# Moving the scale-and-shift products of the first stage onto the matrix engine, and one gate chunk into another buffer

## The chip, the cores and the metric

The kernel runs on one core of one Trainium2 chip. The metric is the device time of one execution in microseconds (us). The engines of the core work side by side and wait for each other through semaphores: TensorE (PE in the profile; PEld is its weight load), VectorE (DVE), ScalarE (ACT), GpSimd (POOL), and SyncE (SP), which in this kernel only issues transfers (DMAs).

## The reference

One layer of a hybrid backbone: 1024 latent tokens and 128 context tokens, 1024 channels, float32. What matters here is its beginning, and one branch:

```python
mod = silu(cond) @ w_mod + b_mod
shift, scale, gate = split(mod, 3)
h = layernorm(x) * (1 + scale) + shift
proj = h @ w_in                      # q, k, v, z of an attention and a retention branch
...
g = sigmoid(h @ w_gate + b_gate)     # two gates of 1024 channels each
m = ga * oa + gr * orr               # oa, orr: the two branches
out = m @ w_out
y = layernorm(ALPHA * x + gate * out) * ln_g + ln_b
```

`cond` has two rows, one for the latent tokens and one for the context tokens. So scale and shift are two vectors of 1024 each.

## The kernel before, in words

Everything is transposed: the 1152 tokens lie along the free axis, the channels in eight blocks (`KT`) of 128 partitions. `Y` holds h, split into a high and a low part (`Y[:, 0, k]` and `Y[:, 1, k]`), and every matrix multiplication with h or a weight is three float32r products: high by high, low weight by high h, high weight by low h. A weight tile of 128x1024 is split likewise into `whi` (ScalarE, `hi_of`, line 156) and `wlo` (`lo_of`: subtraction on GpSimd, line 185, or on VectorE, line 164). The 1152 tokens are worked in three chunks of 384 columns (`CW`).

Instructions are issued in the order in which the program writes them, on each engine. From `sch.run` on, a planner (`Sched`) chooses the order of several streams from estimated costs (`sch.op`, and `sch.t` for TensorE); the first stage, `phase_h`, is written out by hand. Its order:

1. SyncE's queue loads `cond`, x tile 0, the identity, the bias `bm`, then x tiles 1 to 8 (512 KB each). The tiles use six buffers (`p0x`), two buffers of `pz`, and one weight buffer (`raw`); a later load into a `p0x` buffer waits in the queue until its last reader is done.
2. `stats` (VectorE, with `rstd_of` on GpSimd) and `normalise` (VectorE or ScalarE, the string `by`) per tile. `cond_rows`: TensorE broadcasts silu(cond) over 128 partitions, ScalarE copies it to `scb`.
3. Per tile, eight TensorE transposes into two banks (`tp`), and two ScalarE copies into `xnT`.
4. Scale and shift of a block of 128 channels come in two ways. `by_rows`: VectorE multiplies a 128x1024 weight tile (channels on partitions) by `scb` and sums along the row, for both rows of `cond`; this serves scale blocks 0 and 1 and all eight shift blocks. `scale_k` and `scale_cols`: TensorE multiplies with silu(cond) as a stationary operand of two columns, ScalarE copies the two rows out, TensorE turns them into columns, VectorE adds the bias; this serves scale blocks 2 and 3 (`GS[0]`) and 4 to 7 (`GS[1]`), between or after the other work.
5. The weights of the first two jobs (`first`: q and k of the retention branch's first pair) are split, the low parts on GpSimd.
6. `mod(j)` makes block j of h: ScalarE scales and shifts (`hf`), ScalarE rounds to the high part, GpSimd (block 7: VectorE) subtracts for the low part. `k_part` runs block k's products of both first jobs, all three chunks of both jobs accumulating in six banks.
7. The last two blocks are done per job (`last_parts`). ScalarE copies out the first job's result (`qz`), and the dense stream starts with the next job.

In `phase_a` (retention, and the attention's q, k and v) and `phase_b` (attention, gates, output) the dense stream runs a job per weight tile: each of its three chunks uses one of two banks (`dn`), and its evacuation frees the bank. `g_job` is a gate block: ScalarE applies tanh into a buffer `gt` (two buffers) and the chunk is stored to DRAM. `gate_out` and the rope of `qk_job` use the two buffers `tz`. The first two gate jobs run where `phase_a` ends and `phase_b` begins.

Of the kernel before, what the change touches and what calls it, by code (L numbers as in the profile page):

```python
# [18 lines left out]
P = 128  # L19
# [120 lines left out]
def hybrid_step(ctx: ExitStack, tc: tile.TileContext, I: dict, O: dict):  # L140
# [114 lines left out]
    class Job:  # L255
# [12 lines left out]

        def split(self, eng="p"):
            for i, r in enumerate(self.raw):  # L270
                pool = self.pool2 if i else wp
                h = pool.tile([P, 1024], F32R, tag="whi", name="whi")
                l = pool.tile([P, 1024], F32R, tag="wlo", name="wlo")
                f = hi_of(h, r)
                self.ready = lo_of(eng, l, r, h, f)
                self.hi.append(h)
                self.lo.append(l)
# [81 lines left out]
    def phase_h(first, load_decays):  # L359
# [3 lines left out]
        with es:  # L363
# [21 lines left out]
            def load_wm(kind, j):  # L385
                t = wm[kind, j] = p0x("wm")
                dma(t, I["w_" + kind][j])


            GS = ((2, 4), (4, KT))  # L390

            def load_wk(g, k):

                a, b = GS[g]
                n = 8 // (b - a)
                t = p0x("wk") if (g, k) in ((1, 4), (1, 6)) else p0.tile([P, D], F32, tag="wk", name="wk", bufs=3)
                t = t.rearrange("p (k c) -> p k c", k=n)
                dma(t, I["w_scale_k"][k:k + n, :, (a - 2) * P:(b - 2) * P].rearrange("k p c -> p k c"))
# [38 lines left out]
            def by_rows(kind, j):  # L437

                d = m1 if kind == "scale" else sh
                for r in range(2):  # L440
                    v_stt(junk, wm[kind, j], 1.0, scb[r], ALU.mult, ALU.mult, accum_out=d[:, j, r:r + 1])
                if kind == "scale":
                    v_ts(d[:, j, :], d[:, j, :], bm[:, 8 + j:9 + j], 1.0, ALU.add, ALU.add)
                else:
                    v_ts(d[:, j, :], d[:, j, :], bm[:, j:j + 1], None, ALU.add)
# [3 lines left out]
            def scale_k(g, k):  # L449

                n = (GS[g][1] - GS[g][0]) * P
                if k == 0:
                    scale_ps[g] = psum_now("tp")
                mm(scale_ps[g][0:2, :n], sc[:, k, :], wm[g, k], k == 0, k == KT - 1)

            def scale_cols(g):
                a, b = GS[g]
                rows = p0.tile([2, 512], F32, tag="rows", name="rows")
                act(rows[:, :(b - a) * P], scale_ps[g][0:2, :(b - a) * P])
                tp = psum_now("tp")  # L460
                for j in range(b - a):
                    nc.tensor.transpose(tp[:, 2 * j:2 * j + 2], rows[:, j * P:(j + 1) * P], ident[0:2, 0:2])
                    sch.t += 0.107
                v_stt(m1[:, a:b, :], tp[:, 0:2 * (b - a)].rearrange("p (j r) -> p j r", r=2), 1.0,
                      bm[:, 8 + a:8 + b].rearrange("p (j o) -> p j o", o=1).to_broadcast([P, b - a, 2]),
                      ALU.add, ALU.add)
# [66 lines left out]
            def k_part(n, k, part):  # L533
                hi, lo = vw[n]
                for c in range(NC):
                    ps, cs = acc[n][c][:, :CW], slice(c * CW, (c + 1) * CW)
                    if part == 0:
                        mm(ps, hi[0][:, k, :], Y[:, 0, k, cs], k == 0, False)
                        mm(ps, lo[0][:, k, :], Y[:, 0, k, cs], False, False)
                    else:  # L540
                        mm(ps, hi[0][:, k, :], Y[:, 1, k, cs], False, k == KT - 1)

            for k in range(KT - 2):
                mod(k + 1)
                for part in range(2):
                    for n in range(2):
                        k_part(n, k, part)
                if k < 3:
                    for q in range(3 * k, min(3 * k + 3, KT)):
                        scale_k(1, q)  # L550
                if k == 2:
                    scale_cols(1)
# [4 lines left out]
        def last_parts(n):  # L557
            for k in (KT - 2, KT - 1):
                for part in range(2):
                    k_part(n, k, part)  # L560
# [412 lines left out]
    def phase_b():  # L973
# [584 lines left out]
def _layout(a):  # L1558
# [13 lines left out]
    out["w_scale"] = wm[:, D:D + 2 * P].T.reshape(2, P, D)  # L1572
# [55 lines left out]
```

## Time and profile before

| | |
|---|---|
| median of 3 runs | 1702.33 us (1699.15 to 1705.84) |
| profiled execution | 1701.82 us, of which the span is 1700.0 us |
| TensorE busy | 1654.5 us (97%) |
| VectorE, ScalarE, GpSimd busy | 856.3, 609.6, 813.1 us |
| chain that ended last | PE 80%, DVE 6%, DMA 5%, POOL 3%, ACT 2% of the span |

The span is the time from the first to the last recorded instruction; the time of the execution also has what lies around it. "Busy" counts an engine's instructions, "idle before" is the engine's idle time ahead of an instruction and what ended it. The chain is found by going back from the last instruction, at each step to what released it. The stretches view gives, for each stretch, its length, then the busy time (and number of instructions) of PE, PEld, DVE, ACT and POOL, the clock granted to TensorE as a share of full speed, the busy share of the transfer engines and GB/s.

### The profile page before, as it was taken

What the parts mean: (1) busy time and instruction counts of PE and PEld (TensorE: products, weight loads), DVE (VectorE), ACT (ScalarE), POOL (GpSimd) and SP (SyncE); (2) the same over time, 40 slices, a digit from 0 to 9 for tenths busy, and PEclk for the clock granted to TensorE, in tenths of its full rate; (3) what the DMA queues carried; (4) which work ended last, traced back from release to release, by engine and by line L of the source; (5) the groups of instructions that cost most, each with busy time, mean ns of one, the idle gap of its engine ahead of it and who ended that gap; (6) DMA issues with size and microseconds to landing.
All of it is one profiled execution on the core that took longest, in us unless ns stands there. A gap on an engine that the chain in (4) does not pass through costs nothing.

```text
span 1700.0 us, 27027 instructions
## 1 busy us (share of the span) xinstructions
PE 1654.5 (97%) x10495; PEld 1609.5 (95%) x10495; DVE 856.3 (50%) x1681; ACT 609.6 (36%) x1138; POOL 813.1 (48%) x555
## 2 busy tenths in 40 slices
PE   6899999999999999999999999999999999999998
PEld 5699999999999999999999999999999999999886
DVE  8545506413714626665555665666565124134676
ACT  5632222121221235555555555555545220012200
POOL 4547417444634637664847475656656322112200
PEclk8999999999999999999999999999999999999999
DMA  7435412430341365443535353525242578854432
GB/s 274 149 100 147 131 46 86 132 116 23 100 127 44 112 204 161 152 144 113 169 97 172 92 167 93 170 95 165 75 158 73 202 273 282 260 174 137 160 125 87
DMA packets 135185, 237.36 MB, mean 140 GB/s; under 512 B 15801, under 2 KB 103313, under 8 KB 134033
## 3 DMA queue, kind: packets, MB, share of 16 engines
q1 hardware_dynamic: 135056, 235.63, 43.4%
q8 instruction: 83, 1.36, 0.3%
q14 instruction: 46, 0.37, 0.1%
HBM read 161.08 MB, written 74.49 MB: 139 GB/s over the span
## 4 chain that ended last, share of the span: by engine, by line
PE 80%; DVE 6%; DMA 5%; issue 3%; POOL 3%; ACT 2%; SPq 1%; DVEq 0%; POOLq 0%; ACTq 0%
PE dn L149 53%; PE S L149 8%; PE o L149 6%; PE e L149 6%; PE tp L153 4%; PE a L149 4%; DMA gt<-Gd 2%; DVE junk L173 1%; SPq L203 1%; DMA wm<-in_w_shift 1%; ACT E L156 1%; PE tp L149 1%; DVE st L181 1%; DVE eps L173 1%; POOL wlo L185 1%
## 5 line engine op out<-in xcount | busy, mean ns | idle before, releaser
L149 PE MATMUL dn<-Y,whi 128*128 128x384 f32 x3200 | 834.3, 341 | 8.7 <-ACT Y L156 2.8
L149 PEld LDWEIGHTS dn<-Y,whi 128*128 128x128 f32 x3200 | 568.1, 189 | 14.7 <-ACT Y L156 4.0
L149 PE MATMUL dn<-Y,wlo 128*128 128x384 f32 x1600 | 537.5, 336 | 0.7 <-DVE wlo L164 0.7
L185 POOL TENSOR_TENSOR wlo<-raw,whi 128x1024 fp32r<-128x1024 f32 x87 | 210.9, 2428 | 444.8 <-ACT whi L156 444.5
L149 PEld LDWEIGHTS dn<-Y,wlo 128*128 128x128 f32 x1600 | 301.5, 188 | 1.0 <-DVE wlo L164 1.0
L1067 DVE TENSOR_REDUCE nm<-S 128x1 f32<-128x1152 f32 x144 | 178.1, 1237 | 180.4 <-PE S L149 180.0
L189 POOL TENSOR_SCALAR E<-E,r 128x640 f32<-128x640 f32 x64 | 142.8, 2231 | 126.8 <-DVE r L173 86.2
L156 ACT ACTIVATE E<-S,nm 128x1152 f32<-128x1152 f32 x144 | 162.4, 1128 | 79.4 <-DVE nm L1067 73.5
L149 PE MATMUL dn<-whi,Y 128*128 128x256 f32 x864 | 157.4, 283 | 2.4 <-ACT rt L156 1.0
L149 PEld LDWEIGHTS dn<-whi,Y 128*128 128x128 f32 x864 | 134.1, 189 | 3.3 <-ACT rt L156 1.4
L149 PE MATMUL o<-wTh,V 128*128 128x256 f32 x576 | 133.6, 290 | 0.1
L156 ACT ACTIVATE wTh<-tp 128x512 fp32r<-128x512 f32 (+1 forms) x168 | 88.7, 544 | 111.4 <-PE tp L153 107.7
L156 ACT ACTIVATE whi<-raw 128x1024 fp32r<-128x1024 f32 x88 | 92.1, 1055 | 85.0 <-PE dn L149 84.8
L149 PE MATMUL dn<-wlo,Y 128*128 128x256 f32 x432 | 121.3, 281 | 0.0
L164 DVE TENSOR_TENSOR wTl<-tp,wTh 128x512 fp32r<-128x512 f32 (+1 forms) x168 | 99.7, 613 | 24.9 <-ACT wTh L156 24.9
L185 POOL TENSOR_TENSOR E<-E 128x640 f32<-128x640 f32 x64 | 100.9, 1576 | 5.3
L149 PE MATMUL S<-K,QH 128*128 128x384 f32 (+1 forms) x400 | 94.6, 340 | 5.8 <-ACT E L156 5.8
L149 PEld LDWEIGHTS o<-wTh,V 128*128 128x128 f32 x576 | 99.3, 188 | 0.5 <-ACT wTh L156 0.4
L149 PE MATMUL S<-K,QL 128*128 128x384 f32 (+1 forms) x400 | 92.5, 334 | 0.0
L153 PE MATMUL tp<-ident,E 128*128 128x128 f32 x584 | 86.8, 272 | 0.0
L173 DVE SCALAR_TENSOR_TENSOR gt<-gt,dn 128x384 f32<-128x384 f32 x48 | 26.6, 554 | 117.9 <-DMA gt<-Gd 64.7
L169 DVE TENSOR_SCALAR KD<-tp,kdec 128x256 f32<-128x256 f32 (+1 forms) x48 | 16.0, 408 | 138.5 <-PE tp L153 138.5
(197 smaller groups left out, 2504.4 us busy)
## 6 DMA issues: line engine op xcount, KB each, us to landing
K<-Kd SPq DMA_DIRECT2D x8, 1280.0 KB, 7.9
Gd<-gt SPq DMA_DIRECT2D x48, 192.0 KB, 2.3
V<-Vd SPq DMA_DIRECT2D x24, 384.0 KB, 3.6
gt<-Gd SPq DMA_DIRECT2D x48, 192.0 KB, 2.5
Y<-OAd SPq DMA_DIRECT2D x16, 576.0 KB, 4.2
raw<-in_w_gate SPq DMA_DIRECT2D x16, 512.0 KB, 4.0
QH<-Qh SPq DMA_DIRECT2D x64, 128.0 KB, 3.1
QL<-Ql SPq DMA_DIRECT2D x64, 128.0 KB, 2.9
```

Of the source, the lines that this page charges most:

```text
L149: nc.tensor.matmul(out, lhsT=lhsT, rhs=rhs, start=start, stop=stop)
L153: nc.tensor.transpose(out, in_, ident)
L156: nc.scalar.activation(out, in_, func, **kw)
L164: nc.vector.tensor_tensor(out, a, b, op=op)
L169: nc.vector.tensor_scalar(out, a, s1, s2, op0=op0, **kw)
L173: nc.vector.scalar_tensor_tensor(out, a, s, b, op0=op0, op1=op1, **kw)
L181: nc.vector.bn_stats(out, a)
L185: nc.gpsimd.tensor_tensor(out, a, b, op=op)
L189: nc.gpsimd.tensor_scalar(out, a, s1, None, op0=op0)
L203: nc.sync.dma_start(out=out, in_=in_)
L1067: nc.vector.tensor_reduce(nm[:, m:m + 1], ps[:, :nb, :kw], axis=AX.XY, op=ALU.max, negate=True)
```

## The change

The order of the first loads, the place where the first blocks' scale and shift are computed, who splits and subtracts, and one buffer:

- `w_mod01` is a new layout of the input: scale and shift of blocks 0 and 1 side by side, 512 columns, with the contraction index on partitions. Its four tiles are loaded between the x tiles. `cond` is loaded behind x0, the identity and the bias behind x1.
- `GS` now has three groups: the 512 columns of `w_mod01`; scale 2 and 3; scale 4 to 7. Group 0's `scale_k` products stand between the transposes of tiles 1 to 6, its `scale_cols` behind tile 6. Groups 1 and 2 stand behind the first part of blocks 0 and 1.
- `by_rows` is left for the shifts of blocks 2 to 7.
- `split` is divided into `split_hi` and `split_lo`. The first jobs' low parts, and all low parts of h, are computed by VectorE.
- Block 0's scaling is done on VectorE, in four pieces; its high part in three.
- `k_part` has three parts instead of two (the low weight's products are now a part of their own).
- The decay parameters are loaded at block 2.
- In `g_job`, the middle chunk of the first two gate jobs uses a `tz` buffer.

```diff
+        def split_hi(self, i=0):
+            self.hi.append((self.pool2 if i else wp).tile([P, 1024], F32R, tag="whi", name="whi"))
+            self.ready = hi_of(self.hi[i], self.raw[i])
+
+        def split_lo(self, eng="p", i=0):
+            self.lo.append((self.pool2 if i else wp).tile([P, 1024], F32R, tag="wlo", name="wlo"))
+            self.ready = lo_of(eng, self.lo[i], self.raw[i], self.hi[i], self.ready)
...
-            GS = ((2, 4), (4, KT))
+            GS = ((0, 4), (0, 2), (2, 6))
...
-                t = p0x("wk") if (g, k) in ((1, 4), (1, 6)) else p0.tile([P, D], F32, tag="wk", name="wk", bufs=3)
+                t = p0x("wk") if k == 6 or g == 1 else p0.tile([P, D], F32, tag="wk", name="wk", bufs=3)
...
+            load_x(0)
             dma(cond, I["cond"])
-            load_x(0)
+            load_x(1)
             dma(ident, I["ident"])
             dma(bm, I["b_mod"])
-            for i in range(1, NTILE):
+            load_wk(0, 0)
+            for i in range(2, NTILE):
                 load_x(i)
+                if i in (2, 4, 6):
+                    load_wk(0, i)
...
+                for k in ((), (0, 1), (2,), (3,), (4,), (5,), (6, 7), (), ())[i]:
+                    scale_k(0, k)
+                if i == 6:
+                    scale_cols(0)
+                if i == 7:
+                    first[0].split_hi()
                 if i == 2:
-                    load_wm("scale", 0)
-                    load_wm("shift", 0)
                     first[0].load()
                     first[1].load()
-                    for k in range(0, KT, 4):
-                        load_wk(0, k)
-                    load_wm("scale", 1)
-                    load_wm("shift", 1)
-            first[0].split()
-            first[1].split()
-            for k in range(KT):
-                scale_k(0, k)
-            load_wm("shift", 2)
-            for k in range(0, KT, 2):
-                load_wk(1, k)
-            load_decays()
-            by_rows("scale", 0)
-            by_rows("shift", 0)
-            later_loads = [("shift", j) for j in range(3, KT)]
+                    load_shift(2)
+                    load_wk(1, 0)
+                    load_wk(1, 4)
+                    load_shift(3)
+                    for k in range(0, KT, 2):
+                        load_wk(2, k)
 
             def mod(j):
                 hf = pz.tile([P, NT], F32, tag="o_sb", name="hf", bufs=2)
-                for r, (a, b) in enumerate(((0, NL), (NL, NT))):
-                    act(hf[:, a:b], xnT[:, j, a:b], AF.Identity, scale=m1[:, j, r:r + 1], bias=sh[:, j, r:r + 1])
-                hi_of(Y[:, 0, j, :], hf)
-                lo_of("p" if j < KT - 1 else "v", Y[:, 1, j, :], hf, Y[:, 0, j, :])
-                if j + 2 < KT:
-                    by_rows("shift", j + 2)
-                    if later_loads:
-                        load_wm(*later_loads.pop(0))
-
-            by_rows("scale", 1)
-            by_rows("shift", 1)
+
+                def affine(c0, c1, r):
+                    x, m, b = xnT[:, j, c0:c1], m1[:, j, r:r + 1], sh[:, j, r:r + 1]
+                    if j:
+                        act(hf[:, c0:c1], x, AF.Identity, scale=m, bias=b)
+                    else:
+                        v_ts(hf[:, c0:c1], x, m, b, ALU.mult, ALU.add, fast=True)
+
+                if j:
+                    affine(0, NL, 0)
+                    affine(NL, NT, 1)
+                    hi_of(Y[:, 0, j, :], hf)
+                else:
+                    affine(0, CW, 0)
+                    affine(CW, 2 * CW, 0)
+                    first[0].split_lo("v")
+                    affine(2 * CW, NL, 0)
+                    affine(NL, NT, 1)
+                    for c in range(NC):
+                        hi_of(Y[:, 0, j, c * CW:(c + 1) * CW], hf[:, c * CW:(c + 1) * CW])
+                    first[1].split_hi()
+                    first[1].split_lo("v")
+                if 2 <= j < KT - 2:
+                    by_rows(j + 2)
+                lo_of("v", Y[:, 1, j, :], hf, Y[:, 0, j, :])
+                if j < 2:
+                    by_rows(j + 2)
+                if j in (0, 2):
+                    load_shift(2 * j + 4 - j)
+                    load_shift(2 * j + 5 - j)
+                if j == 2:
+                    load_decays()
+
             mod(0)
-            scale_cols(0)
...
             for k in range(KT - 2):
                 mod(k + 1)
-                for part in range(2):
+                for part in range(3):
                     for n in range(2):
                         k_part(n, k, part)
-                if k < 3:
-                    for q in range(3 * k, min(3 * k + 3, KT)):
-                        scale_k(1, q)
-                if k == 2:
-                    scale_cols(1)
+                    if part == 0 and k < 2:
+                        for q in range(KT):
+                            scale_k(k + 1, q)
+                        scale_cols(k + 1)
...
         def g_job(j):
             def evac(c, ps):
-                t = pz.tile([P, CW], F32, tag="gt", name="gt", bufs=2)
+                if j < 2 and c == 1:
+                    t = pz.tile([P, CW], F32, tag="tz", name="gt", bufs=2)
+                else:
+                    t = pz.tile([P, CW], F32, tag="gt", name="gt", bufs=2)
...
-    out["w_scale"] = wm[:, D:D + 2 * P].T.reshape(2, P, D)
+    out["w_mod01"] = np.concatenate([wm[:, D:D + 2 * P], wm[:, :2 * P]], axis=1).reshape(8, P, 4 * P)
```

More of the change, by code (lines that the diff above doesn't have):

```diff
@@ L267, in load @@
                 self.raw.append(r)
-        def split(self, eng="p"):
[L270 to L277, printed above, removed]
+        def split_hi(self, i=0):
[4 more added lines that the diff above has]
+            self.ready = lo_of(eng, self.lo[i], self.raw[i], self.hi[i], self.ready)
+        def split(self, eng="p"):
+            for i in range(len(self.raw)):
+                self.split_hi(i)
+                self.split_lo(eng, i)
         def views(self):
@@ L383, in load_x, with load_shift @@
                 xt.append(t)
-            def load_wm(kind, j):
-                t = wm[kind, j] = p0x("wm")
-                dma(t, I["w_" + kind][j])
-            GS = ((2, 4), (4, KT))
+            def load_shift(j):
+                t = wm["shift", j] = p0x("wm")
+                dma(t, I["w_shift"][j])
+            GS = ((0, 4), (0, 2), (2, 6))
             def load_wk(g, k):
@@ L395, in load_wk @@
                 n = 8 // (b - a)
-                t = p0x("wk") if (g, k) in ((1, 4), (1, 6)) else p0.tile([P, D], F32, tag="wk", name="wk", bufs=3)
+                t = p0x("wk") if k == 6 or g == 1 else p0.tile([P, D], F32, tag="wk", name="wk", bufs=3)
                 t = t.rearrange("p (k c) -> p k c", k=n)
-                dma(t, I["w_scale_k"][k:k + n, :, (a - 2) * P:(b - 2) * P].rearrange("k p c -> p k c"))
+                dma(t, I["w_scale_k" if g else "w_mod01"][k:k + n, :, a * P:b * P].rearrange("k p c -> p k c"))
                 for i in range(n):
                     wm[g, k + i] = t[:, i, :]
+            load_x(0)
             dma(cond, I["cond"])
-            load_x(0)
+            load_x(1)
             dma(ident, I["ident"])
             dma(bm, I["b_mod"])
-            for i in range(1, NTILE):
+            load_wk(0, 0)
+            for i in range(2, NTILE):
                 load_x(i)
+                if i in (2, 4, 6):
+                    load_wk(0, i)
             junk = p0.tile([P, D], mybir.dt.bfloat16, name="junk")
@@ L435, in cond_rows, with by_rows @@
                     act(scb[r][:, g * 512:(g + 1) * 512], ps)
-            def by_rows(kind, j):
-                d = m1 if kind == "scale" else sh
+            def by_rows(j):
                 for r in range(2):
[L441 to L445, printed above, removed]
+                    v_stt(junk, wm["shift", j], 1.0, scb[r], ALU.mult, ALU.mult, accum_out=sh[:, j, r:r + 1])
+                v_ts(sh[:, j, :], sh[:, j, :], bm[:, j:j + 1], None, ALU.add)
             scale_ps = {}
@@ L452, in scale_k @@
                 if k == 0:
-                    scale_ps[g] = psum_now("tp")
+                    scale_ps[g] = psum_now("tp" if g else "dn")
                 mm(scale_ps[g][0:2, :n], sc[:, k, :], wm[g, k], k == 0, k == KT - 1)
             def scale_cols(g):
-                a, b = GS[g]
+                n = GS[g][1] - GS[g][0]
                 rows = p0.tile([2, 512], F32, tag="rows", name="rows")
-                act(rows[:, :(b - a) * P], scale_ps[g][0:2, :(b - a) * P])
+                act(rows[:, :n * P], scale_ps[g][0:2, :n * P])
                 tp = psum_now("tp")
-                for j in range(b - a):
+                for j in range(n):
                     nc.tensor.transpose(tp[:, 2 * j:2 * j + 2], rows[:, j * P:(j + 1) * P], ident[0:2, 0:2])
                     sch.t += 0.107
-                v_stt(m1[:, a:b, :], tp[:, 0:2 * (b - a)].rearrange("p (j r) -> p j r", r=2), 1.0,
-                      bm[:, 8 + a:8 + b].rearrange("p (j o) -> p j o", o=1).to_broadcast([P, b - a, 2]),
-                      ALU.add, ALU.add)
+                for j0, dst, a, m, one in (((0, m1, 0, 2, 1.0), (2, sh, 0, 2, 0.0)), ((0, m1, 2, 2, 1.0),),
+                                           ((0, m1, 4, 4, 1.0),))[g]:
+                    c0 = 8 + a if one else a
+                    v_stt(dst[:, a:a + m, :], tp[:, 2 * j0:2 * (j0 + m)].rearrange("p (j r) -> p j r", r=2), one,
+                          bm[:, c0:c0 + m].rearrange("p (j o) -> p j o", o=1).to_broadcast([P, m, 2]),
+                          ALU.add, ALU.add)
             def normalise(i):
@@ L538, in k_part @@
                         mm(ps, hi[0][:, k, :], Y[:, 0, k, cs], k == 0, False)
+                    elif part == 1:
                         mm(ps, lo[0][:, k, :], Y[:, 0, k, cs], False, False)
@@ L558, in last_parts @@
             for k in (KT - 2, KT - 1):
-                for part in range(2):
+                for part in range(3):
                     k_part(n, k, part)
```

## The prediction

> **What bounds the kernel now.** I read the page's first part, then the busy time by stretches, the chain of work that ended last, and each engine's timeline of the first stage. The page first, then stretches (PE busy first; granted clock, DMA share and GB/s last):
>
> ```profile
> span 1700.0 us, 27027 instructions
> PE 1654.5 (97%) x10495; PEld 1609.5 (95%) x10495; DVE 856.3 (50%) x1681; ACT 609.6 (36%) x1138; POOL 813.1 (48%) x555
> ...
> 0.00:75.10 75.10, 55.96 (x268) 41.67 (x269) 58.49 (x91) 41.88 (x56) 39.81 (x35) 0.93 0.57 208
> 200.00:400.00 200.00, 199.22 (x1404) 198.43 (x1403) 58.66 (x162) 47.58 (x94) 78.93 (x56) 1.00 0.30 93
> ```
>
> TensorE is the bound: between 200 and 400 us it is busy 199.22 of 200. In the first 75.10 us it is busy only 55.96, so some 19 us of waiting stand there. Only removed TensorE waiting, or slow TensorE time, can shorten the kernel. Two places hold it. The chain (start, us, what):
>
> ```profile
> 35.75 13.42 DMA wm<-in_w_shift
> ...
> 603.60 7.32 DMA Gd<-gt
> ```
>
> The first stage is led by VectorE's row products (`junk`) and by late loads of their weights; at 603.60 the first gate chunk's store holds its buffer. The timelines (start, duration; in brackets the idle time before and what ended it):
>
> ```profile
> 5.30 6.15 PE L149 MATMUL a<-ident,sc 128*128 128x128 f32 x32 [5.30 <-DMA ident<-in_ident]
> 18.95 3.14 PE L153 MATMUL tp<-ident,xt 128*128 128x128 f32 x16 [0.52 <-ACT xnT L156]
> 25.74 1.14 PE L153 MATMUL tp<-ident,raw 128*128 128x128 f32 x8 [0.20 <-ACT xnT L156]
> 27.08 3.62 PE L149 MATMUL tp<-wk,sc 128*2 128x256 f32 x16 [0.20 <-ACT xnT L156]
> 35.23 0.69 PE L149 MATMUL dn<-Y,whi 128*128 128x384 f32 x1
> 41.15 2.74 PE L149 MATMUL tp<-wk,sc 128*2 128x512 f32 x6
> 67.69 0.33 PE L149 MATMUL dn<-Y,wlo 128*128 128x384 f32 x1
> 67.86 0.33 PE L149 MATMUL dn<-Y,whi 128*128 128x384 f32 x1
> 80.51 0.44 PE L149 MATMUL dn<-Y,wlo 128*128 128x384 f32 x1 [0.69 <-DVE wlo L164]
> ...
> 7.78 1.29 DVE L181 BATCH_NORM_STATS2 st<-xt 128x6 f32<-128x512 f32 x2 [1.27 <-DMA xt<-in_x]
> 9.23 0.76 DVE L169 TENSOR_SCALAR xt<-xt,mv,rs 128x1024 f32<-128x1024 f32 x1
> 29.52 2.18 DVE L169 TENSOR_SCALAR sh<-sh,bm 128x2 f32<-128x2 f32 x1
> 31.62 1.21 DVE L173 SCALAR_TENSOR_TENSOR junk<-wm,scb 128x1024 bf16<-128x1024 f32 x1
> 32.88 3.25 DVE L173 SCALAR_TENSOR_TENSOR junk<-wm,scb 128x1024 bf16<-128x1024 f32 x1
> 73.19 1.36 DVE L164 TENSOR_TENSOR Y<-hf,Y 128x1152 fp32r<-128x1152 f32 x1 [3.25 <-ACT Y L156]
> 79.23 1.22 DVE L164 TENSOR_TENSOR wlo<-raw,whi 128x1024 fp32r<-128x1024 f32 x1 [4.69 <-ACT whi L156]
> ...
> 21.28 1.23 ACT L156 ACTIVATE xt<-xt,rs 128x1024 f32<-128x1024 f32 x1
> 26.43 1.09 ACT L156 ACTIVATE xnT<-tp 128x512 f32<-128x512 f32 x2 [0.26 <-PE tp L153]
> 27.41 1.99 ACT L156 ACTIVATE whi<-raw 128x1024 fp32r<-128x1024 f32 x2
> 31.80 1.62 ACT L156 ACTIVATE hf<-xnT,sh,m 128x1024 f32<-128x1024 f32 x2 [2.40 <-DVE sh L169]
> 33.46 1.16 ACT L156 ACTIVATE Y<-hf 128x1152 fp32r<-128x1152 f32 x1
> 56.16 0.59 ACT L156 ACTIVATE rows<-tp 2x512 f32<-2x512 f32 x1 [0.95 <-PE tp L149]
> 75.09 1.98 ACT L156 ACTIVATE qz<-dn 64x384 f32<-64x384 f32 x4 [1.93 <-PE dn L149]
> ...
> 28.54 6.50 POOL L185 TENSOR_TENSOR wlo<-raw,whi 128x1024 fp32r<-128x1024 f32 x2 [4.98 <-ACT whi L156]
> ```
>
> Read in order: the transposes end at 26.9 (25.74 + 1.14), but the first projection starts only at 35.23. Between lie the row products for block 0's scale and shift, the shift's bias add (2.18 us beside GpSimd's split, where another product takes 1.21 alone and 3.25 beside one), 1.62 of scaling, 1.16 of high part. Projections are spaced 67.86 - 67.69 = 0.17 us. The stage's end is q's first evacuation at 75.09; the next job's weights then follow on ScalarE and VectorE (1.22 at 79.23), and the stream starts at 80.51.
>
> **The change, part by part.** *Loads.* The same 27 tiles of 512 KB, in another order: the four tiles of scale and shift 0 and 1 stand among the x tiles. Clock and transfer rows:
>
> ```profile
> 17.00:19.00 2.00, 1.48 (x9) 1.05 (x7) 1.97 (x6) 1.98 (x4) 1.04 (x3) 0.51 1.03 410
> 21.00:23.00 2.00, 1.07 (x8) 0.60 (x6) 1.81 (x4) 2.00 (x4) 1.16 (x3) 1.00 1.08 353
> 35.00:37.00 2.00, 2.00 (x7) 1.98 (x8) 1.96 (x3) 0.00 (x0) 2.00 (x2) 0.50 0.05 2
> 60.00:63.00 3.00, 0.57 (x5) 0.25 (x3) 2.93 (x6) 2.87 (x4) 0.01 (x1) 1.00 0.00 0
> ...
> 609.00:611.60 2.60, 0.00 (x1) 0.00 (x0) 0.00 (x0) 0.58 (x2) 0.00 (x0) 0.87 1.03 381
> 611.60:613.00 1.40, 1.35 (x4) 1.35 (x5) 0.00 (x0) 1.40 (x2) 0.38 (x1) 0.50 0.50 179
> 617.00:618.00 1.00, 1.00 (x5) 1.00 (x4) 0.00 (x0) 0.00 (x0) 0.00 (x0) 0.61 1.15 312
> ```
>
> At 410 GB/s a tile takes 1.28 us. x1 lands at 7.78 (the DMA wait ends there); the last x tile is now the 13th, so 7.78 + 11 x 1.28 = 21.9. Its statistics (1.29 and the aggregation) end at 23.4, which hides in what follows. SP's queue now stops at the fourth of these tiles until x0 is transposed (about 15), with x7, x8 and both first weights behind it; what is queued ahead (seven x and three weight tiles) keeps the transfers busy to about 17, and x7 joins the queue before it runs dry: nil to 0.5 us, my estimate. `ident` moves behind x1, from 5.30 to about 7.7 (x1's landing, which no longer waits for `ident`'s 64 KB); that delays the conditioning broadcasts, 6.15 us ending at 11.45 now, to 13.85. It costs 2.4 us of TensorE time before transpose 0, and I count all of it. `cond` moves behind x0; `sc` is still ready before `ident`. `load_decays` and shifts 4 to 7 go later on SP, needed first after the stage.
>
> *Scale and shift 0, 1 on TensorE.* Six products at 41.15 took 2.74 and belong to three k: spaced 0.43, so 0.87 per k of 512 columns. Eight k add 6.9 us between the transposes. Removed: eight 256-wide k (3.62 at 27.08) and eight 1.21 us row products, with their reads and bias adds about 10.2 us of VectorE. TensorE chain: transposes 1.05 a tile; 13.85 + seven tiles 7.4 + 6.9 + waits for evacuations 0.2 ends at 28.3. Then `scale_cols`: copy 0.59, four small transposes 0.4, two tiny VectorE adds, with hand-offs to 29.8; its accumulator lies in a bank of `dn` that nothing wants yet. Behind these adds on VectorE stands tile 8's normalisation (0.76 to 30.55), behind the column transposes those of tile 7. Tile 7's and 8's transposes end 31.65; ScalarE's whi split (half of 1.99, now ahead of tile 8's evacuation) and 1.09 evacuation end 33.2. Covered by this: the ScalarE normalisations (1.23).
>
> *Block 0 in pieces.* VectorE scales the first 768 columns, and splits q's weights, while ScalarE evacuates. A 1024 piece takes 0.76, so 384 about 0.35. After 33.2 only one 384-wide high part remains, 0.5 (a third of 1.16 and overhead): first projection at 33.75, against 35.23, with 2.1 us idle before it. Later pieces and k's weight split keep the second half until 35.75.
>
> *From there TensorE leads.* 144 projections in the stage, 18 of them after its critical point: 126 x 0.1735 = 21.9 us. Second scale group 3.5, third 7.0, each with a copy and column transposes and hand-offs (0.75 and 1.1), 1.2 us of waits in block 0: 35.4 in all, end 33.75 + 35.4 = 69.2. VectorE is next: it gets eight low parts of 1.36 and two of 1.22 from GpSimd, and has six shifts' products (about 2.5 each) left, now alone on its memory (the 3.25 shrinks to 1.21). The third group's columns come at 33.75 + 24 projections 4.2 + 10.5 + hand-offs and waits 3.1 = 51.6; from 52, three shifts 7.5 and five low parts 6.8 make 66.3, and the last low part, which waits for ScalarE's high part, ends near 68; it is needed at 69.0. The second group's scales stand on VectorE behind the row products of shifts 2 and 3, so block 2 starts on ScalarE only at 45; the third group's 7.0 us on TensorE, to 51, cover that. So what VectorE takes over from GpSimd costs nothing as long as this 1 us holds; without it, 1 to 2 us. Loads of shift 5 wait for row product 2 (41) and land by 45, needed 52. ScalarE has 2.8 per block against 3.1 of projections.
>
> q's evacuation then starts at 69.3 instead of 75.09: gain 5.8. What follows keeps its length (80.51 - 75.09 = 5.42). Bounds: 1.5 if the stage keeps its length from the first projection on (33.75 against 35.23); with `ident` arriving as before, 8.2.
>
> *Gate chunk in z's buffer.* ScalarE and TensorE there:
>
> ```profile
> 600.72 0.58 ACT L156 ACTIVATE gt<-dn,bg 128x384 f32<-128x384 f32 x1 [1.87 <-PE dn L149]
> 611.02 0.58 ACT L156 ACTIVATE gt<-dn,bg 128x384 f32<-128x384 f32 x1 [9.72 <-DMA Gd<-gt]
> ...
> 611.65 1.01 PE L149 MATMUL dn<-Y,whi 128*128 128x384 f32 x2 [2.65 <-ACT gt L156]
> ```
>
> Chunk 2 needs chunk 0's buffer, whose store lands at 610.9 (603.60 + 7.32). TensorE idles 2.65, and its clock then stands at 0.50 to past 617: some 5.8 us at half rate, 2.9 lost. With chunk 1 in `tz` (rope, its last reader, comes ahead of the gate chunks), chunk 2 takes the second `gt` as soon as it is computed, 24 projections after chunk 1: 600.7 + 4.2 = 604.9. The next job's first chunk still waits until 611 for chunk 0's store, but TensorE has the other bank to fill to 613. Gain 2.65 + 2.9 = 5.5. Bounds: 0, if another store is then the late one, to 5.5.
>
> Sum against the profiled execution's 1701.82 us (1700.0 span and 1.82 around it; 0.5 under the median 1702.33): -5.8 - 5.5 = 1690.5. The order of later work can shift, since it is planned from costs that change here; where, as between 200 and 400, almost nothing idles, it has little to win or lose, and I allow 2 us either way.
>
> [...] From 18.95 to 22.1 only transposes ran, and the clock went from 0.51 to 1.00. [...]
>
> **Rivals.** *1. A cold start of the projections.* No TensorE work from 30.7 (27.08 + 3.62) to about 35 left the clock at 0.50 at 35.00:37.00, 2.65 us did so at 609, while 60.00:63.00 (0.57 busy of 3.0) kept 1.00. My gap is 2.1 us. If it drops, about 6 us run at half rate: 3 lost, 1693.5. [...]
>
> *2. The gate wait stays*, for another late store: transfers are near saturation there (1.03). Then -5.8 alone: 1696.0. For it: 7.32 us for one store. Against: chunk 2's buffer is untouched until then.
>
> *3. Slower: the clock stays at half from the transposes to block 1.* Place: TensorE's chain, 13.85 to 54. At half rate the 2-column products cost 17.4 more, 72 transposes 4.0 (3.14/16 = 0.196 at 18.95 against 1.14/8 = 0.14), 36 projections 5.3: +27, so 1701.8 + 27 - 11 = 1718. It decides once the extra passes 11 us, that is when the third scale group is cold as well. Against: the products at 27.08, right behind transposes, took 3.62/16 = 0.226, the same per column as those at 41.15; at half the clock it would be 0.45.
>
> *4. The stage gains nothing*, because hand-offs between VectorE, ScalarE and TensorE that I set too short, or loads, make up the 5.8: 1696.3.
>
> **How the numbers follow.** Forecast 0.50 (1688 to 1693.5); rival 1 0.20; rival 2 0.15; rival 4 0.10; rival 3 0.05. 0.5% is 8.5 us, the least that a measurement of this kernel can tell from no change: the line is 1693.8. Faster: 0.50 and half of rival 1, 0.60; slower: 0.05; same 0.35. Range: 1686 (`ident` as early as now and the later order 2 us better: 1690.5 - 2.4 - 2) to 1698 (rival 2 or 4 with the order 2 us worse).
>
> **What would show it.** First projection near 33.8, no GpSimd split before 70, first q evacuation near 69.3, stream start near 74.7; clock 1.00 from 21 us on; no idle TensorE behind the first gate job's `gt`, and clock 1.00 after it. The forecast is wrong if `scale_cols` holds VectorE's queue (tile 8) much past 30, if the projections of blocks 0 and 1 are spaced 0.32, or if VectorE's last low part ends past 69.

## The result, and the profile after

| | before | after |
|---|---|---|
| median, side by side | 1700.9 us (1698.74 to 1705.84, 6 runs) | 1692.26 us (1690.51 to 1694.42, 6 runs) |
| profiled execution | 1701.82 us, span 1700.0 | 1694.42 us, span 1692.6 |

The ratio is 0.9947, 95% interval 0.9931 to 0.9962: faster by 0.53%, 8.6 us, at the edge of the half per cent that the prediction took as its line. The forecast was 1690.5 us, in 1686 to 1698. The profiled execution is the slowest of the six after; what that hides comes below. Of the kernels further down, one run of the gate edit alone (e3) took 2715.07 us at a mean granted clock of 0.556 and is in no ratio. The page of after and its stretches, as shown of before (PE busy first; granted clock, DMA share and GB/s last):

```profile
span 1692.6 us, 27051 instructions
PE 1654.4 (98%) x10515; PEld 1605.9 (95%) x10515; DVE 845.0 (50%) x1676; ACT 608.2 (36%) x1139; POOL 784.5 (46%) x546
...
0.00:70.00 70.00, 58.28 (x288) 39.43 (x289) 47.80 (x86) 40.45 (x57) 11.60 (x26) 0.98 0.64 227
13.00:33.00 20.00, 17.11 (x89) 8.35 (x87) 13.67 (x32) 15.13 (x27) 5.89 (x12) 1.00 1.04 393
33.00:35.00 2.00, 1.34 (x4) 0.83 (x5) 0.61 (x1) 2.00 (x3) 0.00 (x0) 0.81 1.02 389
35.00:37.00 2.00, 2.00 (x7) 0.67 (x6) 2.00 (x3) 1.97 (x3) 0.00 (x0) 0.50 0.14 54
37.00:39.00 2.00, 2.00 (x9) 0.67 (x8) 1.97 (x3) 0.07 (x1) 0.00 (x0) 0.83 0.00 0
609.00:611.60 2.60, 2.60 (x17) 2.60 (x16) 1.30 (x1) 1.85 (x3) 1.35 (x1) 1.00 1.00 356
720.00:725.00 5.00, 2.43 (x13) 2.11 (x12) 0.56 (x1) 2.67 (x5) 3.44 (x3) 0.87 0.60 208
725.00:730.00 5.00, 5.00 (x26) 4.91 (x26) 2.55 (x4) 2.30 (x5) 0.50 (x1) 0.78 0.00 0
```

TensorE's busy time is what it was (1654.4 against 1654.5), so on balance the 7.4 us of span are waiting that went. The first stage is 58.28 busy in 70. From 13 to 33 us the clock is 1.00, with nothing but transposes and two-column products until the first projection at 32.45; between 33 and 39 it falls to 0.50; at 609 TensorE no longer waits; at 720 to 730 there is a new loss. The timelines of the first stage (start, duration; idle time and its end in brackets):

```profile
7.03 5.39 PE L149 MATMUL a<-ident,sc 128*128 128x128 f32 x32 [7.03 <-DMA ident<-in_ident]
14.68 1.88 PE L149 MATMUL dn<-wk,sc 128*2 128x512 f32 x4
29.64 1.14 PE L153 MATMUL tp<-ident,raw 128*128 128x128 f32 x8 [0.23 <-ACT xnT L156]
32.45 0.86 PE L149 MATMUL dn<-Y,whi 128*128 128x384 f32 x2 [1.67 <-ACT Y L156]
35.67 4.58 PE L149 MATMUL tp<-wk,sc 128*2 128x256 f32 x16
75.33 0.44 PE L149 MATMUL dn<-Y,wlo 128*128 128x384 f32 x1 [0.64 <-DVE wlo L164]
...
28.55 0.80 DVE L169 TENSOR_SCALAR raw<-raw,mv,rs 128x1024 f32<-128x1024 f32 x1
67.28 1.36 DVE L164 TENSOR_TENSOR Y<-hf,Y 128x1152 fp32r<-128x1152 f32 x1 [1.63 <-ACT Y L156]
...
69.96 1.98 ACT L156 ACTIVATE qz<-dn 64x384 f32<-64x384 f32 x4 [2.71 <-PE dn L149]
...
76.38 4.77 POOL L185 TENSOR_TENSOR wlo<-raw,whi 128x1024 fp32r<-128x1024 f32 x2 [8.05 <-ACT whi L156]
```

The transposes end at 30.78, the first projection starts at 32.45 (35.23 before), the stream at 75.33 (80.51 before): a lead of 5.18. At 14.68 stand two k of the scale products, between transposes; no GpSimd split comes before 76.38. The first gate job, after, on ScalarE:

```profile
593.47 0.56 ACT L156 ACTIVATE gt<-dn,bg 128x384 f32<-128x384 f32 x1
600.10 0.58 ACT L156 ACTIVATE gt<-dn,bg 128x384 f32<-128x384 f32 x1 [3.58 <-PE dn L149]
```

Chunk 2 follows at 600.10, where before it waited for the store until 611.02. Matching the same instruction in both traces gives the lead along the kernel (ScalarE's gate chunk and softmax rows):

| instruction | before, us | after, us | lead |
|---|---|---|---|
| stream start | 80.51 | 75.33 | 5.18 |
| first gate chunk | 598.28 | 593.47 | 4.81 |
| first softmax | 620.85 | 610.33 | 10.52 |
| softmax rows at about 696 and 734 us of after | | | 10.73, then 7.75 |
| end of the span | 1700.0 | 1692.6 | 7.4 |

So 10.7 us were won by 700 us, close to the 11.3 of the sum, and 3.0 were lost at one place, 722 us. Behind it smaller steps nearly cancel: 1.3 more went at 990 us, and 1.0 came back between 1440 and 1500. The chain of waits, SyncE, ScalarE and TensorE there:

```profile
713.96 8.26 DMA ORd<-goh
...
713.27 0.59 SPq L203 DMA_DIRECT2D K<-Kd  x1
...
722.24 0.49 ACT L156 ACTIVATE goh<-dn 128x384 f32<-128x384 f32 x1 [2.68 <-DMA ORd<-goh]
723.98 1.33 PE L149 MATMUL S<-K,QH 128*128 128x384 f32 x3 [2.57 <-ACT E L156]
```

A chunk of the retention branch's gated output (`gate_out`; "the reset gate" in the expectations below) is stored from a `goh` buffer; there are two. The store was issued 0.7 us behind the 1280 KB load of the third head's K, and landed after 8.26 us. ScalarE's copy into that buffer waited 2.68, the softmax behind it on ScalarE's queue was late, TensorE idled 2.57 us, and its clock went to 0.87 and 0.78 in the two rows above. Before has the same order and the same wait, smaller:

```profile
724.66 6.74 DMA ORd<-goh
...
730.00:735.00 5.00, 3.95 (x26) 3.60 (x25) 1.45 (x3) 2.94 (x6) 4.13 (x4) 1.00 0.71 239
```

There the store took 6.74, TensorE lost about 1.05 of the 5 us at 730 to 735, and the clock stayed at 1.00. So about half of the 3.0 us is the longer wait (2.57 - 1.05 = 1.5), and the rest is the slow clock behind it.

### The profile page after: what moved, and what is told of

Same layout as the page of the kernel before. It is cut to its first block, busy times and chain, and to the rows that moved or that the text cites. A ratio compares the mean times of both kernels' runs of the same rounds, so it can differ in the third digit from the quotient of the medians.

```text
span 1692.6 us, 27051 instructions
## 1 busy us (share of the span) xinstructions
PE 1654.4 (98%) x10515; PEld 1605.9 (95%) x10515; DVE 845.0 (50%) x1676; ACT 608.2 (36%) x1139; POOL 784.5 (46%) x546
## 4 chain that ended last, share of the span: by engine, by line
PE 86%; issue 3%; DVE 3%; DMA 3%; POOL 3%; ACT 2%; SPq 0%; DVEq 0%; POOLq 0%; ACTq 0%
PE dn L149 56%; PE S L149 8%; PE o L149 6%; PE e L149 6%; PE a L149 5%; PE tp L153 5%; PE tp L149 1%; DMA gt<-Gd 1%; ACT E L156 1%; DMA Vd<-vh 1%; POOL wlo L185 1%; DMA ORd<-goh 0%; SPq L203 0%; DVE eps L173 0%; DMA RSd<-rst 0%
## 5 line engine op out<-in xcount | busy, mean ns | idle before, releaser
L185 POOL TENSOR_TENSOR wlo<-raw,whi 128x1024 fp32r<-128x1024 f32 x85 | 204.5, 2409 | 434.5 <-ACT whi L156 432.3
```

What stands on the lines that cost most here:

```text
L185: nc.gpsimd.tensor_tensor(out, a, b, op=op)
```

## The experiments

Each kernel is compared with runs of the kernel before on the same chip. These gave medians of 1699.43 us (e1 to e4), 1700.58 (e5 to e8) and 1702.32 (e9 to e12, on another chip), so kernels of different groups are compared by their ratios and not by their times. Theory: two gains, 5 to 6 us in the first stage and 5 to 6 at the gate, which add up, less what a transfer takes back at 722 us. Rival: one of them is the whole gain, or the first stage's lead is lost on the way.

**The changed kernel again, and each half alone.**

> The changed kernel once more, as it is. Theory: 1692 us, ratio 0.993 to 0.996. In its first profile the lead over the kernel before was 10.5 us at the first softmax (610 us) and 7.4 us at the end; 3 us went at 722 us (a store of the gated output took 8.3 us, TensorE idled 2.6 us and its clock fell) and at 990 us. The order of the instructions there is that of the kernel before. Theory A: such a loss belongs to one execution; the second profile has another pattern and a lead nearer 9 to 11 at the end. Rival B: it comes from the shifted transfers and is there again, 2.6 us of TensorE waiting for E near 722.

1692.21 us, ratio 0.9957 [0.9945, 0.9969]. The profiled execution has the loss at 722 us once more (store 8.48 us, TensorE idle 2.79), as rival B said.

```diff
 # e2: this edit, in the changed kernel; e3: the kernel before, with the lines marked - in place of the one marked +
-                if j < 2 and c == 1:
-                    t = pz.tile([P, CW], F32, tag="tz", name="gt", bufs=2)
-                else:
-                    t = pz.tile([P, CW], F32, tag="gt", name="gt", bufs=2)
+                t = pz.tile([P, CW], F32, tag="gt", name="gt", bufs=2)
```

> The changed kernel with both gate jobs' middle chunks back in gt: the first stage's part alone. Theory (two gains that add): stage lead 5.2 at the stream's start (75.3 us), TensorE again idle 2 to 3 us at the third gate chunk and at half clock behind it; 5.5 us slower than the changed kernel, 1697.5 us, ratio 0.997. Rival: the wait at the gate came from the old timing of the first stage and does not return: 1692, ratio 0.995.

> The kernel before with the gate edit alone. Theory: the wait of 2.65 us and the half clock behind it go, nothing else: 5.5 us faster than before, 1695.5 us, ratio 0.9968. Rival (another store is the next late one): 0 to 2.7 us faster.

The first stage alone: 1700.89 us, ratio 1.0001 [0.999, 1.0012], nothing, where 0.997 was expected. The gate edit alone: 1696.48 us, 0.9978 [0.9969, 0.9988], some 3.7 us, where 0.9968 was expected, just outside this interval. In e3's trace the lead goes from -0.7 at the first gate chunk to +5.0 at the first softmax: 5.7 us, the predicted 5.5. In e2's, the stage's lead is there at the gate (593.78, 4.5 ahead), and goes in two steps:

```profile
608.36 1.01 PE L149 MATMUL dn<-Y,whi 128*128 128x384 f32 x2 [3.82 <-ACT gt L156]
...
721.16 8.73 DMA ORd<-goh
...
731.66 1.33 PE L149 MATMUL S<-K,QH 128*128 128x384 f32 x3 [3.05 <-ACT E L156]
```

The wait for the gate chunk's buffer is 3.82 instead of 2.65, which leaves 3.3 of the lead; and at 722 to 732 the store takes 8.73, TensorE idles 3.05 and its clock falls: the lead goes from 3.5 to -1.1. The two halves don't add in the medians: 0 and 3 us alone, 7 to 9 together.

**The identity early.** The prediction counted 2.4 us for the later identity.

```diff
-            load_x(0)
             dma(cond, I["cond"])
-            load_x(1)
+            load_x(0)
             dma(ident, I["ident"])
+            load_x(1)
```

> The changed kernel with the identity loaded behind x0 again, and cond first, x1 and the bias behind them. Theory (TensorE's chain leads the transposes, and the identity starts it): identity at 5.3 instead of 7.0, first projection 1 to 1.7 us earlier (near 31), the kernel 1 to 2 us faster than the changed one, ratio 0.994. Rival (the x tiles' landing leads, as VectorE's waits of 0.2 to 0.7 us for them say): first projection as now at 32.4, 1692 us.

1691.91 us, ratio 0.995 [0.9938, 0.9962]. The identity is there at 5.17 (7.03), yet the first projection comes at 31.99, only 0.46 earlier, closer to the rival: VectorE now waits 1.40 us for x tile 2 (0.68 in after), so the tiles' arrival, more than the identity, sets the pace. The stream starts at 74.75. The lead is 10.9 at the first softmax and stays at 11.1 past 722 us:

```profile
713.52 6.83 DMA ORd<-goh
...
722.11 0.79 PE L149 MATMUL S<-K,QH 128*128 128x384 f32 x3 [1.14 <-ACT E L156]
```

The same order of the queue, and here the store takes 6.83 and TensorE idles 1.14.

**The K load later.** Is the loss at 722 us due to this load?

```diff
-                if c == 1:
+                if c == 1 and h != 1:
                     load_k(h + 1)
...
                 for t in range(2 if lat else 1):
                     yield ...
+                    if h == 1 and c == 1 and t == 1:
+                        load_k(h + 1)
```

> The changed kernel with one transfer issued later: the third head's K load (1280 KB) goes behind two pairs of the reset gate's stores instead of ahead of them (at about 724 instead of 713.27 us); all else as it was. Theory A (3 us of the lead are lost at 722 us because the goh store stands behind the K load and takes 8.3 to 8.5 us, so ScalarE's copy into its buffer is late, TensorE idles 2.6 to 2.8 us and its clock falls): the store takes about 3 us, the copy does not wait for it, no half clock at 720 to 730, the lead over before stays near 10.5 us past 735, and the time is 2.5 to 3.5 us under the changed kernel, about 1689.3 (ratio to before 0.9935 to 0.994). Theory B (the K load only moves the collision to the next store or the lead is lost elsewhere on the way): no more than 1 us under the changed kernel, 1691.5 to 1692.5, with a wait of the same size between 725 and 760 us.

> The later K load as in e5_late_k_load, with the first stage changed and the gate chunk left as before. With the early K load this kernel was no faster than before (1700.89). Theory A (the first stage does give some 4.5 us; 1.2 of them go to a longer wait for the gate chunk's buffer and 3 to 4.6 to the store behind the K load): the 4.6 us at 722 us come back, 1696.5 to 1698 (ratio 0.9975 to 0.9985). Theory B (the first stage's lead is lost at the transfers whatever their order): 1700 to 1701.5, ratio 1.000.

> The kernel before with the third head's K load issued behind two pairs of the reset gate's stores, as in e5_late_k_load. Theory A (in the kernel before the store takes 6.7 us and TensorE waits 1.05 us for it, with no fall of its clock; only the changed stage shifts the transfers so that 8.3 to 8.7 us and 2.6 to 3 us with a half clock come of it): 1 to 1.5 us faster than before, ratio 0.9988 to 0.9998. Theory B (the order of this load is worth 4 us in any of these kernels, and what it gave without the gate edit says nothing on the first stage): 1696 to 1697, ratio 0.997 to 0.998.

With it the changed kernel took 1691.28 us (0.9948 [0.9933, 0.9964]), the one without the gate edit 1696.12 (0.9978 [0.9965, 0.999], in e6's range A), the kernel before 1698.44 (0.9981 [0.9971, 0.9991]). The wait is gone, as expected, in all three traces: `goh<-dn` waits for no store, and TensorE does not stop. In e5:

```profile
714.05 0.54 SPq L203 DMA_DIRECT2D ORd<-goh  x1
722.28 0.44 SPq L203 DMA_DIRECT2D K<-Kd  x1
...
720.19 0.48 ACT L156 ACTIVATE goh<-dn 128x384 f32<-128x384 f32 x1
...
720.00:725.00 5.00, 5.00 (x34) 4.87 (x33) 3.22 (x4) 3.18 (x7) 4.48 (x4) 1.00 0.53 152
725.00:730.00 5.00, 5.00 (x37) 4.88 (x36) 3.88 (x9) 3.16 (x8) 3.17 (x2) 1.00 0.68 268
```

The clock is 1.00 and PE is busy throughout, where after had 0.87 and 0.78; the lead grows there from 10.0 to 11.3 instead of falling. So e5's theory A was right on the wait, and not on the time. How much the load costs the kernel before isn't settled: e11's ratio, 0.9981 or 3.2 us, lies between its theory A (0.9988 to 0.9998) and its B (0.997 to 0.998) with an interval that reaches both, and its trace gains 1.3 us at this place, the size of A.

By the ratios e5 is at most 1.5 us under the changed kernel, not the expected 3. Two things bear on that. The wait is not the same in every execution: in the ten traces with the early load TensorE idled 1.02, 1.05, 1.14, 1.26, 1.35, 1.57, 2.27, 2.57, 2.79 and 3.05 us there. The clock fell behind the last three alone; e10, with 2.27 us and no fall, lost 1.2 us of its lead there. The profiled executions of after and e1, with 2.57 and 2.79, were the slowest of their kernels (1694.42 in 1690.51 to 1694.42, 1695.47 in 1691.02 to 1695.47), but e2's, with 3.05, was not (1701.36 in 1694.44 to 1703.54). And the clock can fall elsewhere: e5's own trace loses 1.6 us of its lead at 1127 us, behind a pause of 1.23 us that does no such harm in most other traces (last section). That such chance losses hide the 3 us in e5's median is argued, not shown. What makes the store take 6.7 or 8.7 us in the same order of transfers stays open.

**The clock at the first projection.** Two of the second group's products are moved ahead of it:

```diff
+            for q in range(2):
+                scale_k(1, q)
...
-                        for q in range(KT):
+                        for q in range(0 if k else 2, KT):
                             scale_k(k + 1, q)
```

> The changed kernel with two of the second group's eight scale and shift products moved ahead of the first projection, into TensorE's wait for h's first block. Theory A (the pause of 1.67 us there is what lets the clock fall to 0.50 to 0.81 at 33 to 38 us, and that costs about 2 us): the granted clock stays at 1.00 from 20 to 40 us, the second group's products end about 2 us sooner, and the projections stream from about 73 instead of 75.3 us; 1690 to 1691. Theory B (VectorE and the arrival of weights set the stream's start, TensorE has slack in this stage): clock 1.00 as well, but the last low part of h still ends at 68 to 69 us, the stream starts at 75 us, and the time stays within 1 us of the changed kernel.

1692.44 us, ratio 0.9956 [0.9942, 0.9971]: no difference that the medians show. The trace shows one:

```profile
33.00:35.00 2.00, 1.84 (x7) 0.64 (x4) 0.94 (x3) 1.93 (x5) 0.00 (x0) 1.00 1.02 389
35.00:37.00 2.00, 1.50 (x7) 0.82 (x8) 1.52 (x2) 1.97 (x4) 0.00 (x0) 1.00 0.14 54
...
29.05 0.40 PE L467 MATMUL tp<-ident,rows 2*128 2x2 f32 x4 [0.68 <-ACT rows L156]
32.65 1.02 PE L149 MATMUL tp<-wk,sc 128*2 128x256 f32 x4 [0.78 <-ACT xnT L156]
36.23 2.75 PE L149 MATMUL tp<-wk,sc 128*2 128x256 f32 x12
74.06 0.44 PE L149 MATMUL dn<-Y,wlo 128*128 128x384 f32 x1 [0.64 <-DVE wlo L164]
```

The clock stays at 1.00; TensorE's wait there is 0.78. The wait of 1.67 or 1.68 stands in seven traces (after, e1, e2, e4, e5, e6, e8), and the clock fell behind it in all seven; with 0.78 (e7, e12) it fell in neither. In the execution of e7 the column transposes came at 29.05 (27.96 after); counted from them the second group ends 9.93 us later (12.29 after: 35.67 + 4.58 - 27.96) and the stream starts 45.01 later (47.37). Of these 2.36 us some 0.9 are the two products (a quarter of 3.62) that now lie in the wait, 1.5 the clock: 7.18 instead of 7.71 us to the rest of the group, and 1.0 in the group itself (4.58 for sixteen products against 3.62 before). Theory A in the trace, B in the medians.

**Who makes the low parts.** In the changed kernel they go back to GpSimd (e8), and in the kernel before they go to VectorE (e9):

```diff
 # e8, changed kernel; both first jobs likewise: split_lo("v") to split_lo("p")
-                lo_of("v", Y[:, 1, j, :], hf, Y[:, 0, j, :])
+                lo_of("p" if j < KT - 1 else "v", Y[:, 1, j, :], hf, Y[:, 0, j, :])
 # e9, kernel before; both first jobs likewise: split() to split("v")
-                lo_of("p" if j < KT - 1 else "v", Y[:, 1, j, :], hf, Y[:, 0, j, :])
+                lo_of("v", Y[:, 1, j, :], hf, Y[:, 0, j, :])
```

> The changed kernel with the low parts of h's blocks 0 to 6 and of the first two weight chunks back on GpSimd, where before had them; scale and shift still by TensorE, first block in pieces, gate chunk in z's buffer. Theory A (before, a VectorE step beside a GpSimd split took 2.2 to 3.5 us instead of 0.23 to 1.22, six times, 13 us in all, and that was a term of the old stage): about five VectorE steps are stretched by 2 us each where VectorE itself would have spent 1.3 us, the stream starts 3 to 5 us later than 75.3, and the time is 1694 to 1697. Theory B (what sets the start of the stream is TensorE's scale and shift products and ScalarE's blocks; VectorE has idle time of 4.6 us at 48 us to take the stretch): stream start within 1 us of 75.3, time within 1 us of the changed kernel.

> The kernel before, with the low parts of h's blocks 0 to 6 and of the first two weight chunks on VectorE instead of GpSimd; scale and shift stay on VectorE as they were, the gate chunk too. Theory A (the GpSimd splits are the larger term of the first stage: each stretches a VectorE step beside it by about 2 us, and putting them back into the changed kernel moved the stream of projections from 75.3 to 79.5 us): no VectorE step of 2 us or more in 28 to 70 us, the stream starts at 76 to 78.5 instead of 80.5 us, with no help of TensorE. Theory B (the scale and shift sums on VectorE are the term, and 11 us of low parts added to them take as long as the stretch of 13 us that goes): the stream starts at 80 to 82 us. For the time, since a lead at the start alone has been lost at the gate chunk and at the third head's K load: 1697 to 1700 under A, 1700 to 1702 under B.

e8: 1695.53 us, ratio 0.9973 [0.9961, 0.9985], some 3 to 4 us behind the changed kernel, and its stream starts at 79.50, 3.45 later if counted from the column transposes (28.68). Seven VectorE steps are stretched; two of them, and what TensorE waits for:

```profile
38.84 7.25 POOL L185 TENSOR_TENSOR Y<-hf,Y 128x1152 fp32r<-128x1152 f32 x2
...
40.06 3.51 DVE L173 SCALAR_TENSOR_TENSOR junk<-wm,scb 128x1024 bf16<-128x1024 f32 x1
43.62 2.50 DVE L169 TENSOR_SCALAR sh<-sh,bm 128x2 f32<-128x2 f32 x1
...
71.95 0.62 PE L149 MATMUL dn<-Y,whi 128*128 128x384 f32 x2 [1.40 <-POOL Y L185]
```

A row product takes 3.51 instead of 1.21, and the two-column sum behind it 2.50 instead of 0.23. GpSimd's low part of block 6 ends last: TensorE waits 1.40 for it at 71.95. Both stretched steps run while GpSimd makes two low parts (38.84 to 46.09); why they are stretched, and whether it is the memory that the prediction names, no run shows.

e9 went against its theory A, and past its B (stream at 80 to 82 us): 1705.12 us, ratio 1.0015 [1.0004, 1.0025], slower.

```profile
28.79 2.36 DVE L164 TENSOR_TENSOR wlo<-raw,whi 128x1024 fp32r<-128x1024 f32 x2 [4.26 <-ACT whi L156]
36.59 1.62 ACT L156 ACTIVATE hf<-xnT,sh,m 128x1024 f32<-128x1024 f32 x2 [6.89 <-DVE sh L169]
40.02 0.69 PE L149 MATMUL dn<-Y,whi 128*128 128x384 f32 x1
85.00 0.44 PE L149 MATMUL dn<-Y,wlo 128*128 128x384 f32 x1 [0.64 <-DVE wlo L164]
```

No step is stretched, but the two weight splits (2.36 us) now stand on VectorE's queue ahead of block 0's row products, and VectorE idles 4.26 us for their high parts first: the row products begin at 31.06 instead of 24.32. ScalarE's scaling waits for them until 36.59 (31.80), TensorE idles 8.74 and the first projection comes at 40.02 (35.23), the stream at 85.00 (80.51). So taking the splits from GpSimd is worth 3.5 us in the changed kernel, where TensorE took block 0's sums from VectorE, and costs 4.5 in this order without that. Splits issued behind block 0's row products were not tried.

**Block 0 in one piece,** on ScalarE:

```diff
-                    if j:
-                        act(hf[:, c0:c1], x, AF.Identity, scale=m, bias=b)
-                    else:
-                        v_ts(hf[:, c0:c1], x, m, b, ALU.mult, ALU.add, fast=True)
+                    act(hf[:, c0:c1], x, AF.Identity, scale=m, bias=b)
...
-                    for c in range(NC):
-                        hi_of(Y[:, 0, j, c * CW:(c + 1) * CW], hf[:, c * CW:(c + 1) * CW])
+                hi_of(Y[:, 0, j, :], hf)
```

> The changed kernel with h's first block applied and rounded in one piece on ScalarE (1152 columns) instead of pieces on VectorE and ScalarE. Theory A (the pieces let the first projection begin before the block is complete, and TensorE is the chain from 28 to 52 us): the first projection starts 1.5 to 3 us later than 32.5, its wait grows from 1.7 to 3 to 4.5 us, the half clock behind it lasts longer, and the stream starts 2 to 3.5 us later than 75.3; 1693 to 1696. Theory B (the first weight chunk's arrival at 34.2 us holds the second pair of products anyway): first projection later, second group of scale products and stream within 0.7 us of the changed kernel, time within 1 us.

1695.42 us, ratio 0.9964 [0.9953, 0.9976]; that it is slower than the changed kernel is not certain by these intervals.

```profile
28.30 0.40 PE L467 MATMUL tp<-ident,rows 2*128 2x2 f32 x4 [0.68 <-ACT rows L156]
35.09 1.01 PE L149 MATMUL dn<-Y,whi 128*128 128x384 f32 x2 [3.97 <-ACT Y L156]
76.50 0.45 PE L149 MATMUL dn<-Y,wlo 128*128 128x384 f32 x1 [0.64 <-DVE wlo L164]
```

The first projection is 2.3 us later (counted from the column transposes, 0.34 later here), the stream only 0.83. In after the last three of the first six products waited for k's weights anyway; here all six run in one go. So the trace is nearer to theory B, and the median lies in A's range. The pieces gain the start and give most of it back.

**All three edits together** (identity early, two products first, K load later).

> The changed kernel with three edits of the earlier runs together: the identity and the condition loaded ahead of x, two products of the second group ahead of the first projection, and the third head's K load behind two store pairs. Theory A (the three losses are at different places and add up): stream of projections from 73 to 74 us, clock 1.00 from 20 to 40 us, lead over before 12 to 13 us at the first softmax, the same past 735 us, 1687.5 to 1689.5, ratio 0.992 to 0.9935. Theory B (short waits elsewhere that halve the clock, at another place in each execution, decide the median): lead of 12 us at the first softmax too, lost again by 2 to 4 us at some later place, 1690.5 to 1692, ratio 0.994 to 0.9955.

1688.31 us (1687.16 to 1689.15, 4 runs), ratio 0.9918 [0.9904, 0.9931], its interval at the edge of the changed kernel's (0.9931). The stream starts at 72.65, the clock is 1.00 from 13 to 43 us, the lead is 14.1 at the first softmax and 15.6 past 722 us: theory A, with a larger lead than it gave. By the ratios this is 5 to 7 us under the changed kernel, though none of the three edits alone moved a median clearly (e4 0.995, e7 0.9956, e5 0.9948); with four runs, why they give more together stays open.

## Why the prediction was right

- *The identity* came at 7.03, not 7.7, and the broadcasts ended at 12.42, not 13.85. Cost: not the 2.4 us counted but about 0.5 (e4), as the x tiles set the pace.
- *Scale and shift on TensorE:* 1.88 us for two k, 0.94 each against 0.87. The transposes ended at 30.78 (forecast 31.65), VectorE's tile 8 normalisation at 29.35 (30.55), the first projection came at 32.45 (33.75), after a gap of 1.67 (2.1 forecast).
- *The clock.* Rival 1 happened: 0.81, 0.50, 0.83 from 33 to 39 us. It cost about 1.5 us (e7); the rival said 3. The second group took 4.58 instead of 3.5. That miss and the first projection, 1.3 us early, nearly cancel, which is luck.
- *VectorE as the next limit:* its last low part ended at 68.64 (forecast 68, needed at 69). It took over the splits at no cost to TensorE, whose only wait of over 0.2 us between 41 and 73 us (0.68, at 51.98) ends on ScalarE; e8 shows what they cost on GpSimd, 3.5 us.
- *The stage:* first evacuation 69.96 (69.3), stream 75.33 (74.7); 5.1 to 5.2 us instead of 5.8.
- *The gate chunk:* 5.7 us against 5.5, in the traces of after and e3 measured against that of before. That size belongs to an execution in which the clock fell behind the wait: in e11, the same program up to there, TensorE waited 3.17 us, its clock stayed at 1.00, and the stretch cost 2.3 us less. The ratio of e3 gives 3.7 us, with an interval from 2.0 to 5.3, so 5.5 was high for the usual execution.
- *Rival 3* is out: no run shows the half clock from the transposes to block 1 that its 1718 takes; from 13 to 33 us the clock was 1.00 in after, e4 to e8, e10 and e12. *Rival 2* is out: no wait, clock 1.00 at 609.
- *Rival 4, the stage gains nothing,* is not wholly out. With the gate edit the stage is worth 0.9978 less 0.9947 to 0.9957, 3.6 to 5.3 us. Without it the medians show none: 1.0001 (e2), and 0.9978 against 0.9981 with the late K load (e6, e11), though the e6 and e11 traces differ by 4.0 us of span (1693.1 and 1697.1). The intervals allow 2 to 3 us on each side. What takes the stage's lead in those executions, beyond the gate chunk's longer wait (3.82 in e2 and e6, 2.65 in before, 3.17 in e11), stays open.
- *The order of later work,* allowed 2 us either way, was the term that was mis-sized most: 3.0 us in the profiled execution, at 722 us. "Between 200 and 400, almost nothing idles" was true, and the loss lay outside that stretch, in a wait that the trace of before showed with 1.05 us.

So the sum was 11.3, the trace had 10.7 of it at 700 us, and 8.6 (7.2 in e1) arrived in the medians. The time itself came closer, 1692.26 against 1690.5, because the kernel before took 1700.9 side by side and not the 1701.82 that the sum starts from: 0.9 us of luck.

## What to carry to other kernels

A lead won early can go at any place where a store must land before a buffer is used again, as 3.0 of 10.7 us did at 722 us here: list the waits that end on a transfer all along the kernel, not only those of the changed stage, and add to each what the clock can lose behind it (about 1.5 us there). Moving the splits off GpSimd, beside which a VectorE row product took 3.51 us instead of 1.21, paid once VectorE had been relieved (3.5 us, e8), and not when they were put ahead of VectorE's own urgent work (4.5 us lost, e9). Where one profile per kernel is at hand, a wait of 1 us in it may be 3 us in another (1.02 to 3.05 us at one place in ten traces here), and the clock may fall in one of them and not in the other (behind 2.57 us in after, not behind 2.27 in e10): a term read from one profile has the chance of that execution in it.

## What was not expected of the hardware

- In these traces the length of a TensorE pause does not decide alone whether the clock falls. All fourteen traces have the same pause of 1.23 or 1.24 us at 1121 to 1142 us; behind it the clock stood at 0.50 in e5 and e9, and at 1.00 in the other twelve. In e11 a pause of 3.17 us left it at 1.00, while 2.57 us (after, 722 us) did not. The pause and the clock behind it, e5 and then e11:

```profile
1126.25 0.33 PE L149 MATMUL S<-K,QH 128*128 128x128 f32 x1 [1.23 <-ACT E L156]
...
1127.00:1130.00 3.00, 3.00 (x11) 3.00 (x11) 1.43 (x4) 1.34 (x4) 2.92 (x3) 0.50 0.46 129
...
613.78 0.62 PE L149 MATMUL dn<-Y,whi 128*128 128x384 f32 x2 [3.17 <-ACT gt L156]
...
613.00:618.00 5.00, 4.22 (x24) 4.22 (x25) 0.00 (x0) 2.08 (x3) 2.39 (x1) 1.00 0.81 238
```

  So the clock fell behind pauses of 1.23 us (e5, e9), 1.67 (after, at 32.45) and 2.57 (after, at 723.98), all shorter than the 3.17 us behind which it stayed.
- The 192 KB store issued behind the third head's 1280 KB K load on the same queue took 6.7 to 8.7 us in the ten traces with the early load, against a median of 2.2 for such stores in after:

```profile
ORd<-goh SPq DMA_DIRECT2D x24, 192.0 KB, 2.2
```
